# Gate and up of two feed-forwards by seven block products, and down as a pass of its own, in a two-layer diffusion backbone

## The chip, the cores and the metric

The kernel runs on one core of a Trainium2 chip, as one program. The metric is the device time of one execution in microseconds, from the median of several runs. A profile is one further execution that the hardware profiler recorded; its span is the time from its first to its last recorded instruction.

## The reference

The reference is a backbone of two layers over 512 latent tokens and 256 context tokens of width 1024. Layer 0 mixes with a gated MLP and a Hyena convolution, layer 1 with grouped-query attention. Both end in a SwiGLU feed-forward, which is the part that changes. Cut to it:

```python
D_FF = 2816
def swiglu(h, w_gu, w_down):            # w_gu (1024, 5632), w_down (2816, 1024)
    gate, up = jnp.split(h @ w_gu, 2, axis=-1)
    return (jax.nn.silu(gate) * up) @ w_down
...
x = x + g2 * swiglu(modulate(x, norm2_g[layer], sh2, sc2), ffn_w_gu[layer], ffn_w_down[layer])
if not last:
    ctx = ctx + cg2 * swiglu(modulate(ctx, norm2_g[layer], csh2, csc2), ffn_w_gu[layer], ffn_w_down[layer])
return rmsnorm(x, final_g)              # after the last layer
```

`modulate` is an RMS norm whose result is scaled and shifted per column. The feed-forward of layer 0 ("the first" below) works on 768 tokens, six tiles of 128; that of layer 1 ("the second") on the 512 latent tokens, four tiles.

## The kernel before

**Precision.** Every float32 operand of a matrix product is split into a high part, rounded to the format `fp32r`, and a low part, the rest. ScalarE (ACT) makes the high part with a cast, VectorE (DVE) the low part with a subtraction. A product is three matmuls into the same PSUM bank: high by high, high by low, low by high (`mm3`, lines L144, L146 and L148). For weights, `wload` issues a DMA of 512 KB from SyncE's queue (SP, L163) into one of three buffers called `raw`, then casts (`whi`, L166) and subtracts (`wlo`, L167). The ring of three `raw` buffers is used in the order of issue; a load waits until the subtraction that last read its buffer is done. SP's queue is in order as well.

**Filler.** Each `wload` first calls `fill`, which adds one step of a generator: one load of 512 KB of `mod_w` into the same ring (L328) and the matmuls on it (L331) for the conditioning of the next layer. In the first feed-forward 48 such steps are taken.

**A feed-forward.** `norm_hT` takes a token tile at a time: a sum of squares on ACT (L377), a reciprocal root on DVE and GpSimd (POOL, L362), a scaling on DVE (L379), eight transposes on TensorE (L384), scale and shift of the eight 128x128 blocks, four on ACT (L388) and four on DVE (L390), then a cast (L392) and a subtraction (L393) of 128x512, two of each. Its result `hT`, the transposed tokens in high and low parts, has the features on the partitions and the tokens along the columns. Then 11 groups `gi` follow, each of 256 of the 2816 inner columns. A group makes, for each of its two blocks of 128, the gate and the up product over eight k-blocks, with the weights as the stationary and the tokens as the moving operand; the tokens are taken as 384 + 384 columns in the first feed-forward, as 512 in the second (256 + 256 in its first group). Silu on ACT (L964), a multiplication on DVE (L966), the split of the activations (L154, L155), and then at once the group's part of the down product: for each token tile and each half of the 1024 output columns six matmuls of 512 columns (L979), whose bank DVE adds to a sum `fy` in SBUF (L983). In the last group the bank is multiplied by the gate (L906) and added to the residual `xr` (L907). After the second feed-forward comes the final norm (L1147 to L1159), after the first the norm of the attention.

**Order.** The program is one stream per engine, in an order that a scheduler fixed at build time. An engine works its stream in order; semaphores hold an instruction until its operands are there. `project_tm` (L814) is the routine that the mixers' output projections use: all token tiles have a PSUM bank each and the k-blocks of the weights are streamed past them, two k-blocks per load.

## Time and profile before

| what | value |
|---|---|
| time, median of 3 runs | 2107.66 us (2105.82 to 2111.17) |
| time of the profiled execution | 2105.39 us |
| its span | 2103.5 us |
| granted TensorE clock, mean over the span | 0.985 of full speed |
| TensorE matmul busy | 2020.9 us, 96% of the span |
| VectorE, ScalarE, GpSimd busy | 1134.6, 674.6 and 284.8 us |
| first feed-forward, first gate matmul to last down matmul | 869.7 to 1464.1 us |
| second feed-forward, the same | 1726.7 to 2090.0 us |
| end of the span | 2103.5 us |

The profiled execution took 1.9 us more than its span and 2.3 us less than the median of the runs. Busy shares are averages over stages that differ, so what an edit is worth is read from the stage in which it stands. A matmul's recorded duration includes its passage through the array, and matmuls overlap; the pace of a stream is read from one start to the next.

### The profile page before, as it was taken

Reading aid. Unit: us, or ns where it says so; the run is one execution under the profiler, and the core shown is the slowest. Engines: PE = TensorE matmul, PEld = TensorE weight load, DVE = VectorE, ACT = ScalarE, POOL = GpSimd, SP = SyncE. Lnnn points to the kernel's source line nnn. Section 1 sums busy time; section 2 is a strip of 40 time slices with the busy share of each in tenths; the row PEclk is TensorE's granted clock in tenths of the full one; section 3 lists DMA queues with packets and bytes.
Section 4 is the critical chain, followed back from the end, with each engine's and each line's share of the span. In section 5 each row is a group of like instructions: output and inputs, shape, how many; then the busy total and the mean of one; then the engine's idle time right before and its main releaser. Section 6 shows DMA issues by size and latency. Waiting matters only on the chain.

```text
span 2103.5 us, 27501 instructions
## 1 busy us (share of the span) xinstructions
PE 2020.9 (96%) x10875; PEld 1709.1 (81%) x10875; DVE 1134.6 (54%) x1963; ACT 674.6 (32%) x1234; POOL 284.8 (14%) x267
## 2 busy tenths in 40 slices
PE   5899999999999899899999999998989989999997
PEld 2567777899999788788888888997869978888886
DVE  5786173577777742533333333456687644444447
ACT  4654122233333221511111111113567642222222
POOL 3465010012121210200000000003150020000001
PEclk9999999999999999999999999999999999999998
DMA  7664345422222352323333333222220023233331
GB/s 256 217 221 151 108 158 181 168 78 93 79 94 74 109 203 78 121 90 110 118 99 106 120 121 101 62 69 60 61 80 1 31 71 91 81 109 100 91 105 66
DMA packets 170315, 227.77 MB, mean 108 GB/s; under 512 B 8570, under 2 KB 124395, under 8 KB 169931
## 3 DMA queue, kind: packets, MB, share of 16 engines
q1 hardware_dynamic: 169712, 219.95, 33.2%
q0 software_dynamic: 288, 5.90, 0.7%
q8 instruction: 86, 1.41, 0.3%
q14 instruction: 43, 0.34, 0.1%
q10 hardware_dynamic: 186, 0.17, 0.0%
HBM read 204.91 MB, written 21.07 MB: 107 GB/s over the span
## 4 chain that ended last, share of the span: by engine, by line
PE 89%; DMA 4%; DVE 3%; issue 1%; POOL 1%; ACT 1%; SPq 0%; DVEq 0%; POOLq 0%; ACTq 0%
PE pp L144 15%; PE pp L148 15%; PE pp L146 15%; PE pc L979 13%; PE pp L814 11%; PE pc L814 4%; PE pa L331 3%; DMA raw<-in_mod_w 2%; PE pc L144 1%; PE pc L146 1%; PE pc L148 1%; PE pa L148 1%; PE pa L146 1%; PE pa L144 1%; PE pt L1030 1%
## 5 line engine op out<-in xcount | busy, mean ns | idle before, releaser
L166 ACT CAST whi<-raw 128x1024 fp32r<-128x1024 f32 x208 | 216.7, 1051 | 868.0 <-PE pp L146 381.6
L167 DVE TENSOR_TENSOR wlo<-raw,whi 128x1024 fp32r<-128x1024 f32 x208 | 260.8, 1260 | 367.3 <-ACT whi L166 363.8
L144 PE MATMUL pp<-hTh,whi 128*128 128x384 f32 (+2 forms) x1088 | 324.5, 351 | 1.0 <-ACT hTh L392 1.0
L146 PE MATMUL pp<-hTl,whi 128*128 128x384 f32 (+2 forms) x1088 | 323.7, 348 | 0.0
L148 PE MATMUL pp<-hTh,wlo 128*128 128x384 f32 (+2 forms) x1088 | 322.5, 349 | 0.0
L983 DVE TENSOR_TENSOR fy<-pc,fy 128x512 f32<-128x512 f32 x180 | 120.6, 688 | 193.8 <-PE pc L979 193.6
L144 PEld LDWEIGHTS pp<-hTh,whi 128*128 128x128 f32 x1088 | 198.2, 189 | 29.7 <-ACT fa L964 10.9
L148 PEld LDWEIGHTS pp<-hTh,wlo 128*128 128x128 f32 x1088 | 199.7, 189 | 20.4 <-DVE fy L983 4.2
L146 PEld LDWEIGHTS pp<-hTl,whi 128*128 128x128 f32 x1088 | 199.7, 189 | 13.1
L907 POOL TENSOR_TENSOR xr<-xr,nh 128x512 f32<-128x512 f32 x35 | 49.1, 1425 | 915.2 <-DVE nh L906 911.1
L979 PE MATMUL pc<-whi,fasl 128*128 128x512 f32 x440 | 172.3, 392 | 0.2 <-DVE fasl L155 0.2
L979 PE MATMUL pc<-wlo,fash 128*128 128x512 f32 x440 | 172.2, 391 | 0.0
L979 PE MATMUL pc<-whi,fash 128*128 128x512 f32 x440 | 166.2, 394 | 0.0
L144 PE MATMUL pp<-hT,whi 128*128 128x512 f32 (+1 forms) x512 | 135.5, 341 | 0.4 <-ACT whi L166 0.4
L146 PE MATMUL pp<-hT,whi 128*128 128x512 f32 (+1 forms) x512 | 135.7, 340 | 0.0
L148 PE MATMUL pp<-hT,wlo 128*128 128x512 f32 (+1 forms) x512 | 134.8, 340 | 0.0
L979 PEld LDWEIGHTS pc<-whi,fash 128*128 128x128 f32 x440 | 82.1, 188 | 27.1 <-issue 10.1
L331 PE MATMUL pa<-raw,sc 128*32 128x512 f32 x384 | 87.1, 624 | 10.8 <-DMA raw<-in_mod_w 10.7
L979 PEld LDWEIGHTS pc<-wlo,fash 128*128 128x128 f32 x440 | 82.5, 187 | 17.4
L979 PEld LDWEIGHTS pc<-whi,fasl 128*128 128x128 f32 x440 | 82.6, 188 | 16.2 <-DVE fasl L155 0.6
L144 PEld LDWEIGHTS pp<-hT,whi 128*128 128x128 f32 x512 | 79.6, 188 | 15.1 <-issue 2.5
L148 PEld LDWEIGHTS pp<-hT,wlo 128*128 128x128 f32 x512 | 79.6, 189 | 12.0 <-DVE sv L891 0.8
(344 smaller groups left out, 3787.9 us busy)
## 6 DMA issues: line engine op xcount, KB each, us to landing
raw<-in_mod_w SPq DMA_DIRECT2D x96, 512.0 KB
raw<-in_ffn_w_gu SPq DMA_DIRECT2D x88, 512.0 KB
raw<-in_ffn_w_down SPq DMA_DIRECT2D x44, 512.0 KB
raw<-in_even_w_in SPq DMA_DIRECT2D x40, 512.0 KB
G<-G SPq DMA_DIRECT2D x48, 256.0 KB
Gc<-G SPq DMA_DIRECT2D x16, 768.0 KB
raw<-in_even_w_out SPq DMA_DIRECT2D x16, 512.0 KB
dec<-in_k_dec SPq DMA_DIRECT2D x48, 128.0 KB
```

The source lines that it names most:

```text
L144: mm(o, lh, rh, start=start, stop=False)
L146: mm(o, lh, rl, start=False, stop=False)
L148: mm(o, ll, rh, start=False, stop=stop)
L166: self.nc.scalar.copy(hi, raw)
L167: self.nc.vector.tensor_sub(lo, raw, hi.bitcast(F32))
L331: nc.tensor.matmul(ps[32 * j:32 * j + 32, :], self.sc[:, k, :], raw[:, i * 512:(i + 1) * 512], start=k == 0, stop=k == KT - 1, tile_positi ...
L814: self.nc.tensor.matmul(ps, x[:, ts], y[:, a, :], start=k + a == 0 and i == 0, stop=k + a == wk - 1 and i == 2)
L907: (eng or nc.gpsimd).tensor_add(x[:, cs], x[:, cs], tmp)
L979: nc.tensor.matmul(ps, x[:, ts], y[:, 0, cs], start=i == 0 and j == 0, stop=i == 1 and j == 2)
L983: nc.vector.tensor_add(ys[q][:, cs], ps, ys[q][:, cs])
L1030: self.nc.tensor.transpose(ps[:, js], src[:, js], self.eye)
```

## The change

**Gate and up.** The tokens are taken as pairs of tiles, the 1024 features as two halves, and the gate and up weights of one block of 128 inner columns as the two block columns of a 2x2 matrix. The product of two 2x2 block matrices takes eight block products; the changed kernel uses a scheme of seven (that of Strassen, in its form with fewer additions). For each of the 22 blocks `f`, `weight_pairs` loads the gate block and the up block (two loads of 512 KB into the same `raw` ring), forms four sums of halves (two on POOL, two on DVE, each 128x512), and splits 3.5 blocks of 128x1024 worth of operands where the kernel before splits two. `norm_pairs` makes, in place of `hT`, seven operands per pair of tiles: three of them blocks of the tokens as they are, four sums or differences of such blocks (two on DVE, two on POOL), and the high and the low part of each. `gate_up` runs seven products of four k-blocks each, with 384 columns in the first and 256 in the second feed-forward, into four PSUM banks X, Y, Z, W (L1082); adds the banks together on DVE (L1094, L1098, L1099, L1101); applies silu (L1096, L1102) and the multiplications (L1104 on DVE, L1105 on POOL); and stores the two halves of the activation to a DRAM tensor `act` (L1107, SP).

**Down.** It starts when all 22 blocks are stored, with `project_tm` over 22 k-blocks, once for each half of the output columns, all token tiles in PSUM banks. `act` is loaded back through the `raw` ring (L1044) and split; the second feed-forward keeps all 22 split blocks for the second half, the first keeps 12 and loads ten again. The sums in `fy` and DVE's additions to them (L981, L983, L948, L949) go away. `project_tm` works the last four k-blocks of the second half bank by bank, so that the banks finish one after another.

The diff, cut to its core:

```diff
@@ norm_pairs, in place of norm_hT for the feed-forwards
+            for q in pair:
+                nc.scalar.activation(y, x, AF.Square, accum_out=ss)
+                self.rstd(ss, D, EPS)
+                nc.vector.tensor_scalar(y, x, ss, None, op0=ALU.mult)
...
+            put(0, top(h1))
+            put(1, bot(h1))
+            nc.vector.tensor_sub(t1, top(h2), top(h1))
+            nc.vector.tensor_sub(t2, bot(h2), t1)
+            put(3, t1)
+            put(4, t2)
+            nc.gpsimd.tensor_sub(t3, bot(h2), top(h2))
+            nc.gpsimd.tensor_sub(t4, bot(h1), t2)
+            put(5, t3)
+            put(2, bot(h2))
+            put(6, t4)
@@ weight_pairs
+        h0, l0 = split(ra, self.wp, "w", self.wbufs[1])
+        nc.gpsimd.tensor_add(s1, a21, a22)
+        nc.vector.tensor_sub(s2, s1, a11)
+        h1, l1 = split(st, self.wp, "w", self.wbufs[1])
+        nc.gpsimd.tensor_sub(a11, a11, a21)
+        nc.vector.tensor_sub(a12, a12, s2)
+        h2, l2 = split(ra, sp, "s", 2)
+        h3, l3 = split(a22, sp, "v", 1)
@@ gate_up, for f in range(22)
+            prod(X, a11, b11, True, True)
+            nc.scalar.copy(p1, X)
+            prod(W, s1, t1, True, True)
+            nc.scalar.copy(p5, W)
+            prod(Y, s2, t2, True, True)
+            nc.vector.tensor_add(p1, Y, p1)
+            prod(X, a12, b21, False, True)
+            nc.scalar.activation(a[0], X, AF.Silu)
+            prod(Z, s3, t3, True, True)
+            nc.vector.tensor_add(Z, Z, p1)
+            nc.vector.tensor_add(p5, Z, p5)
+            prod(W, s4, b22, False, True)
+            nc.vector.tensor_add(a[1], W, p1)
+            nc.scalar.activation(a[1], a[1], AF.Silu)
+            prod(Z, a22, t4, False, True)
+            nc.vector.tensor_mul(a[0], a[0], Z)
+            nc.gpsimd.tensor_mul(a[1], a[1], p5)
+            for i in range(2):
+                nc.sync.dma_start(acts[f][:, i * n:(i + 1) * n], a[i])
@@ ffn, down
-                        if gi == 0:
-                            nc.vector.tensor_copy(ys[q][:, cs], ps)
-                        elif gi < ng - 1:
-                            nc.vector.tensor_add(ys[q][:, cs], ps, ys[q][:, cs])
+                for cg in range(2):
+                    banks = self.project_tm(lazy, wd, cg * 512, range(ntt), nff, 2 * cg)
+                    for i, ps in enumerate(banks):
+                        self.gated_add(fp, xs[q], ps, gates[q // 4], cg, nc.vector if l and (i == 3 or cg) else None)
```

Three places of the order are shown, all in the second feed-forward. The first is VectorE's stream in the norm. In the kernel before, a piece of it reads as follows (`nxn` is the scaled tile, `nh` a modulated half, `hTl` its low part, `pp` a PSUM bank):

```order
L379 TENSOR_SCALAR nxn_15455<-xr_7602,nss_15454 128x1024
L390 TENSOR_SCALAR nh_15401<-pp_15400,A_2830_15362,modT_7_98 128x128 x2
L393 TENSOR_TENSOR hTl_15361<-nh_15371,hTh_15360 128x4x128
L393 TENSOR_TENSOR hTl_15361<-nh_15383,hTh_15360 128x4x128
L393 TENSOR_TENSOR hTl_15361<-nh_15401,hTh_15360 128x4x128
L390 TENSOR_SCALAR nh_15413<-pp_15412,A_2830_15362,modT_7_98 128x128 x2
```

In the changed kernel the last tile and the operands of the last pair read as follows (`tt` holds a sum of blocks, `Bl` the low part of an operand; the matmuls that open the products need the `Bl` from `nh_2999` of the row marked x2):

```order
L948 TENSOR_SCALAR nxn_15689<-xr_7602,nss_15688 128x1024
L968 TENSOR_TENSOR Bl_15588<-nh_2999_15669,Bh_15587 128x4x128 x2
L959 TENSOR_SCALAR nh_3004_15694<-pp_15695,A_2982_15589,modT_7_98 128x128 x2
L973 TENSOR_TENSOR tt_15717<-nh_3004_15694,nh_2999_15669 128x512
L959 TENSOR_SCALAR nh_3004_15694<-pp_15704,A_2982_15589,modT_7_98 128x128 x2
L974 TENSOR_TENSOR tt_15718<-nh_3004_15694,tt_15717 128x512
L968 TENSOR_TENSOR Bl_15588<-tt_15717,Bh_15587 128x4x128
L968 TENSOR_TENSOR Bl_15588<-nh_3004_15694,Bh_15587 128x4x128
L968 TENSOR_TENSOR Bl_15588<-tt_15718,Bh_15587 128x4x128
L968 TENSOR_TENSOR Bl_15588<-tt_15726,Bh_15587 128x4x128
L968 TENSOR_TENSOR Bl_15588<-tt_15719,Bh_15587 128x4x128
```

A pair now has seven subtractions to low parts in place of four, and two differences of blocks on the same engine.

The second place is VectorE's stream in the steady part of gate and up. In the kernel before, the piece between two runs of `fy` additions reads:

```order
L167 TENSOR_TENSOR wlo_16774<-raw_16771,whi_16773 128x1024
L966 TENSOR_TENSOR fa_16669<-pp_16708,fa_16669 128x512
L167 TENSOR_TENSOR wlo_16810<-raw_16807,whi_16809 128x1024
L155 TENSOR_TENSOR fasl_16735<-fa_16669,fash_16734 128x512
L167 TENSOR_TENSOR wlo_16816<-raw_16813,whi_16815 128x1024
L966 TENSOR_TENSOR fa_16738<-pp_16777,fa_16738 128x512
```

In the changed kernel one block `f` reads (`st` holds two of the sums, `wlo`, `slo` and `vlo` are low parts of weights, `p_` and `fa_` lie in SBUF, `pp` in PSUM):

```order
L1008 TENSOR_TENSOR st_17424<-st_17424,raw_17416 128x512
L1104 TENSOR_TENSOR fa_3235_17187<-fa_3235_17187,pp_17185 128x256
L1012 TENSOR_TENSOR raw_17416<-raw_17416,st_17424 128x512
L1002 TENSOR_TENSOR vlo_17309<-raw_17289,vhi_17308 128x512
L1094 TENSOR_TENSOR p_3256_17318<-pp_17313,p_3256_17318 128x256
L1002 TENSOR_TENSOR slo_17434<-raw_17416,shi_17433 128x1024
L1002 TENSOR_TENSOR wlo_17428<-st_17424,whi_17427 128x1024
L1098 TENSOR_TENSOR pp_17314<-pp_17314,p_3256_17318 128x256
L1099 TENSOR_TENSOR p_3257_17319<-pp_17314,p_3257_17319 128x256
L1002 TENSOR_TENSOR wlo_17550<-raw_17545,whi_17549 128x1024
L1101 TENSOR_TENSOR fa_3255_17317<-pp_17315,p_3256_17318 128x256
```

The eleven instructions of a block stand interleaved with those of the block before it: the low parts and sums of the next weights lie between the additions of the banks.

The third place is SP's queue of loads. In the kernel before, a group of the second feed-forward issues these six:

```order
L163 DMA raw_17312<-in_ffn_w_gu 128x8x128
L163 DMA raw_17344<-in_ffn_w_gu 128x8x128
L163 DMA raw_17381<-in_ffn_w_gu 128x8x128
L163 DMA raw_17413<-in_ffn_w_gu 128x8x128
L163 DMA raw_17449<-in_ffn_w_down 128x1024
L163 DMA raw_17455<-in_ffn_w_down 128x1024
```

In the changed kernel's first half of down it issues, for every two k-blocks, a weight and two activations:

```order
L163 DMA raw_18678<-in_ffn_w_down 128x2x512
L1044 DMA raw_18684<-act_4_2962_15557 128x512
L1044 DMA raw_18693<-act_5_2963_15558 128x512
L163 DMA raw_18720<-in_ffn_w_down 128x2x512
L1044 DMA raw_18726<-act_6_2964_15559 128x512
L1044 DMA raw_18735<-act_7_2965_15560 128x512
```

Each of the three goes to a buffer of its own of the ring, and the next weight needs the buffer of the last one.

## Rows read from the trace of the kernel before

**Rows 1.** the page: busy time by engine, granted clock, chain that ended last

```profile
PE 2020.9 (96%) x10875; PEld 1709.1 (81%) x10875; DVE 1134.6 (54%) x1963; ACT 674.6 (32%) x1234; POOL 284.8 (14%) x267
...
PEclk9999999999999999999999999999999999999998
...
PE 89%; DMA 4%; DVE 3%; issue 1%; POOL 1%; ACT 1%; SPq 0%; DVEq 0%; POOLq 0%; ACTq 0%
```

**Rows 2.** windows by stage: start:end length, busy us by engine, PEclk, DMA share, GB/s

```profile
852.00:869.70 17.70, 11.85 (x67) 6.93 (x65) 14.59 (x34) 13.17 (x30) 2.71 (x3) 0.90 0.77 241
869.70:1464.00 594.30, 594.12 (x3088) 519.91 (x3089) 229.89 (x298) 112.54 (x148) 13.32 (x13) 1.00 0.32 96
1464.00:1474.00 10.00, 4.33 (x23) 3.62 (x22) 9.07 (x15) 7.48 (x16) 8.63 (x8) 0.70 0.32 102
1713.00:1727.00 14.00, 7.34 (x36) 6.18 (x36) 11.19 (x26) 12.10 (x26) 4.62 (x5) 0.76 0.22 75
1727.00:1731.00 4.00, 4.00 (x23) 4.00 (x22) 3.25 (x8) 3.65 (x7) 0.00 (x0) 0.57 0.02 4
1731.00:2090.00 359.00, 358.02 (x1659) 299.36 (x1657) 172.22 (x212) 94.02 (x122) 5.32 (x5) 1.00 0.30 88
```

**Rows 3.** timeline of PE: gate/up with 384, 512 and 256 columns (start, us)

```profile
935.76 0.51 PE L144 MATMUL pp<-hTh,whi 128*128 128x384 f32 x2
...
939.57 0.51 PE L148 MATMUL pp<-hTh,wlo 128*128 128x384 f32 x2
...
1772.72 0.39 PE L148 MATMUL pp<-hTh,wlo 128*128 128x512 f32 x1
...
1774.53 0.39 PE L146 MATMUL pp<-hTl,whi 128*128 128x512 f32 x1
...
1732.72 0.28 PE L146 MATMUL pp<-hTl,whi 128*128 128x256 f32 x1
...
1735.00 0.28 PE L148 MATMUL pp<-hTh,wlo 128*128 128x256 f32 x1
```

**Rows 4.** groups by line and shape, DVE: busy us, mean ns, idle before

```profile
L167 DVE TENSOR_TENSOR wlo<-raw,whi 128x1024 fp32r<-128x1024 f32 x208 | 260.8, 1260 | 367.3 <-ACT whi L166 363.8 <-PE pc L814 2.0
...
L966 DVE TENSOR_TENSOR fa<-pp,fa 128x384 f32<-128x384 f32 x44 | 22.5, 552 | 60.4 <-PE pp L148 60.4
...
L393 DVE TENSOR_TENSOR hTl<-nh,hTh 128x512 fp32r<-128x512 f32 x32 | 21.0, 685 | 4.1 <-ACT hTh L392 3.5
...
L906 DVE TENSOR_TENSOR nh<-pc,gate 128x512 f32<-128x512 f32 x24 | 16.0, 685 | 6.8 <-PE pc L979 4.4 <-PE pc L814 2.0 <-POOL xr L907 0.4
...
L379 DVE TENSOR_SCALAR nxn<-xr,nss 128x1024 f32<-128x1024 f32 x16 | 14.7, 923 | 6.7 <-POOL nss L362 4.0 <-PE pp L384 1.8 <-issue 1.0
...
L390 DVE TENSOR_SCALAR nh<-pp,A,modT 128x128 f32<-128x128 f32 x40 | 13.6, 402 | 0.9 <-issue 0.8 <-ACT nh L388 0.2
...
L1033 DVE TENSOR_TENSOR PTl<-pt,PTh 128x256 fp32r<-128x256 f32 x32 | 13.3, 415 | 0.9 <-ACT PTh L1032 0.9
```

**Rows 5.** groups by line and shape, ACT and POOL

```profile
L166 ACT CAST whi<-raw 128x1024 fp32r<-128x1024 f32 x208 | 216.7, 1051 | 868.0 <-PE pp L146 381.6 <-PE pc L979 120.6 <-PE pc L814 83.3
...
L392 ACT CAST hTh<-nh 128x512 fp32r<-128x512 f32 x32 | 19.0, 625 | 7.1 <-DVE nh L390 7.1
...
L907 POOL TENSOR_TENSOR xr<-xr,nh 128x512 f32<-128x512 f32 x35 | 49.1, 1425 | 915.2 <-DVE nh L906 911.1 <-DVE nss L361 2.8 <-ACT fy L1147 1.4
...
L581 POOL TENSOR_TENSOR ab<-ab,ab 128x256 f32<-128x256 f32 x32 | 27.9, 871 | 22.2 <-DVE ab L576 19.7 <-PE pp L413 1.6 <-DVE rn L603 0.8
```

**Rows 6.** timeline of DVE and POOL, 565 to 571 us

```profile
566.30 1.78 DVE L155 TENSOR_TENSOR Yr0l<-T,Yr0h 128x512 fp32r<-128x512 f32 x1
...
565.33 2.21 POOL L766 TENSOR_TENSOR T<-T,T 128x512 f32<-128x512 f32 x1
```

**Rows 7.** timeline of SP's and PE's queues at 860 us

```profile
860.75 0.33 SPq L328 DMA_DIRECT2D raw<-in_mod_w  x1
...
863.14 1.35 PE L331 MATMUL pa<-raw,sc 128*32 128x512 f32 x4 [4.56 <-DMA raw<-in_mod_w]
```

More of the change, by code (lines that the diff above doesn't have):

```diff
@@ L934, in ffn @@
+    def ffn(self, xs, l):
         nc, A = self.nc, self.A
         ntt = len(xs)
[L936 to L990 removed]
@@ new lines, in gate_up, with prod @@
+    def gate_up(self, fp, sp, b, wgu, acts, n):
+        nc = self.nc
+        b11, b21, b22, t1, t2, t3, t4 = b
+        mm = nc.tensor.matmul
+        def prod(ps, wt, bt, first, last):
+            (wh, wl), (bh, bl) = wt, bt
+            for k in range(4):
+                for i, (x, y) in enumerate(((wh, bh), (wl, bh), (wh, bl))):
+                    mm(ps, x[:, k, :], y[:, k, :], start=first and k == 0 and i == 0, stop=last and k == 3 and i == 2, skip_group_check=not first)
+        for f in range(len(acts)):
+            a11, a12, s1, s2, s3, s4, a22 = self.weight_pairs(sp, wgu, f * P, DFF + f * P)
+            X, Y, Z, W = (self.psA()[:, 0:n] for _ in range(4))
+            a = [self.t(fp, [P, n], F32, f"fa{i}", 2) for i in range(2)]
+            p1 = self.t(fp, [P, n], F32, "p1", 2)
+            p5 = self.t(fp, [P, n], F32, "p5", 2)
+            prod(X, a11, b11, True, True)
[17 more added lines that the diff above has]
+                nc.sync.dma_start(acts[f][:, i * n:(i + 1) * n], a[i])
@@ L1036, in attention_in @@
         nc, A = self.nc, self.A
-        self.hT = self.norm_hT(xs, 1, 1, hp, "hT")
+        with self.pool("an") as yp:
+            self.hT = self.norm_hT(xs, 1, 1, hp, "hT", yp)
         qT = [[[self.t(kvp, [P, 4, P], F32R, f"qT{p}", 8) for p in "hl"] for _ in range(4)] for _ in range(2)]
@@ L1144, in final @@
         if cg == 0:
[L1145 to L1146 removed]
+            self.fss = getattr(self, "fss", {}) | {i: self.t(self.sp, [P, 2], F32, "fss", 4)}
+        ss = self.fss[i]
         nc.scalar.activation(y[:, halves[cg]], x[:, halves[cg]], AF.Square, accum_out=ss[:, cg:cg + 1])
```

165 lines of the change are left out of this document (102 added, 63 removed).

## Prediction

> **What bounds the kernel now.** I read the page first: TensorE is busy 96% of the span, the chain of waits that ended last is 89% TensorE, and the granted clock is at its upper level, 2.4 GHz, in nearly every slice [rows 1]. Busy shares are averages, so the second view is the windows by stage [rows 2]. In the first feed-forward TensorE is busy 594.1 of 594.3 us at full clock, in the second 358.0 of 359.0; VectorE works 230 and 172 us in the same stretches, ScalarE 113 and 94. Both stages are nothing but matmuls in a row, so what they take is number of matmuls times pace, and VectorE has more than half its time to give. The exceptions are the ends. Ahead of the first gate matmul stand a window of 17.7 us with 11.9 us of TensorE work and one of 14.0 us with 7.3; VectorE is busy 14.6 and 11.2 us there. The third view is the pace, in the timeline [rows 3]: from the first to the last row of each stretch, twice 11 steps of 384 columns take 3.81 us, 173 ns each; 8 steps of 512 take 1.81 us, 226 ns each; 19 of 256 take 2.28 us, 120 ns each. The 256-column stream is in the trace only because the second feed-forward's first group is cut in halves, and it is the row that matters most: all of the new gate and up there runs at that width.
>
> **What is removed.** Gate and up before: first feed-forward 22 blocks x 2 parts x 8 k x 3 x 2 column pieces = 2112 matmuls of 384 columns; after, 22 x 7 products x 4 k x 3 = 1848. The difference of 264 at 173 ns is **45.7 us**. Second: 960 of 512 columns and, in the first group, 192 of 256, so 217.0 + 23.0 = 240.0 us; after, 1848 of 256 at 120 ns, 221.8 us: **18.2 us**. Seven eighths would be 30 us of 240; the rest is lost because a matmul of 256 columns is dearer by the column than one of 512 [rows 3]. Down keeps its 1320 matmuls of 512 columns. Conditioning keeps its 48 steps. In all 64 us of TensorE work go away.
>
> The Trainium skill, TensorE: Matmul & The Clock Gate, section Back-to-back issue gap, gives N / 2.4 + 2.5 ns for an isolated matmul at the upper clock: 109, 162.5 and 216 ns for these widths. By that the two terms would be 43 and 27 us. The rows show 11 ns more at each width, a constant that weighs most on narrow matmuls, and they decide.
>
> DVE's 180 additions to `fy` and ten large ones at the end go too; they were hidden and are worth nothing by themselves.
>
> **Gate and up, steady part.** VectorE per block `f`: three subtractions of 1024 columns at 1.26 us, three ops of 512 in SBUF at 0.685, five from PSUM, at 0.415 for 256 columns and 0.552 for 384 [rows 4]. That is 3.78 + 2.06 + 2.08 = 7.9 us against 84 x 0.120 = 10.1 us of TensorE in the second feed-forward, and 8.6 against 84 x 0.173 = 14.5 in the first. ScalarE, with 3.5 casts at 1.05 us per 1024 columns [rows 5] and four ops of a bank that cost no more than the 512-column cast's 0.625 [rows 5], has at most 6.2. POOL has two ops of 512 at 1.43 and one of 256 at 0.87, 3.7 us [rows 5]. So by busy time alone TensorE stays the bound, with 2.2 us to spare in the second feed-forward.
>
> What can use that up is VectorE against POOL. While POOL's op of 2.21 us ran, a VectorE op of 512 columns with both inputs in SBUF took 1.78 us [rows 6] where the same shape takes 0.685 [rows 4]: 1.1 us more; those that read a PSUM bank keep 0.685 (L906, though its partner on POOL follows it closely). If each of POOL's two ops of 512 costs VectorE 1.1 and the one of 256 half of that, a block takes 7.9 + 2.75 = 10.6 us and TensorE waits 0.55 us x 22 = 12 us. But only 5.8 of each 10.1 us are VectorE ops of that kind, so some 1.6 us will be paid, 9.5 in all: hidden, but at 94% in a fixed order of interleaved blocks (second order shown) some waits of TensorE follow. Below, 0; above, 34 us (the second rival). I take **6 us**.
>
> The Trainium skill, SBUF — State Buffer, section SBUF: two separate sides, speaks against this change: GpSimd and VectorE with two SBUF inputs share a port pair under an exclusive lock, and the later one blocks for the whole instruction of the other. The trace agrees in kind (1.78 against 0.685 us); in size it shows half of POOL's time being paid.
>
> In the first feed-forward the engines have 4 us of slack per block, but the ring of three `raw` buffers is shared by two weights and two conditioning loads per block. A load takes 2.4 us from issue to its first matmul [rows 7]. Before, a weight left its buffer after 1.05 + 1.26 us; now the gate block is overwritten in place and stays for cast, POOL's sum, two VectorE ops, a second cast and its subtraction, 1.05 + 1.43 + 0.69 + 0.69 + 1.05 + 1.26 = 6.2 us and whatever it queues for. Two buffers are thus held for half of each 14.5 us, and conditioning matmuls whose load comes late stop the whole TensorE stream, as one did for 4.56 us [rows 7]. Between 0 and 25 us (1.1 us per block); I take **8**.
>
> **The norms.** They stand on the path: TensorE has nothing else then. Second feed-forward, VectorE work before the first product: four scalings at 0.92, 16 modulations at 0.40, and low parts of 0.685, 8 before; after, 14 and four differences, +10 x 0.685 = 6.9 us. The weight sums and splits of the first two blocks go there too, 2 x (3.78 + 3 x 0.685) = 11.7 us where before about three splits of 1.26 did; +7.9. Five low parts come after the first product can start (the first order shown), -3.4. That is 11.4 us on a VectorE that was busy 11.2 of 14.0 us [rows 2]: **+12 us**, between 8 and 16. First feed-forward, six tiles: 21 low parts for 12 and six differences, +15 x 0.685 = 10.3, the weights' +7.9, less 3.4, and 3.1 us of idle VectorE time to absorb some: **+12**, between 6 and 18. The clock's slower stretch after the norm (0.57 granted between 1727 and 1731 us [rows 2], so mostly 1.2 GHz, after a window with TensorE half idle) is paid before as well.
>
> **Down.** Its first matmuls wait for the first weight and activations to be loaded and split: 2.4 + 1.05 + 1.26 us less what the last products cover, 1 to 3 us, twice: **4**. In the second feed-forward's first half, two k-blocks give TensorE 24 x 0.226 = 5.4 us. The loads are 512 KB and twice 256 KB; at the 241 GB/s of the densest window [rows 2] 4.35 us. A buffer is refilled after load, cast and subtraction: at best 2.4 + 1.05 + 1.26 = 4.7 us, and 4.35 + 2.3 + 0.4 = 7.1 where the three loads share the bandwidth (the third order shown). So 0 to 1.7 us for each of 10 such steps; I take the middle, **8 us**. Before, the two down loads of a group stood among four others with 32 us of matmuls to cover them. The first feed-forward has 36 x 0.226 = 8.1 us per step against at most 7.7: hidden. At the hand-over to attention TensorE is busy 4.3 of 10 us already [rows 2]; six banks now finish within some 4 us where they came 2.7 us apart, 0 to 5, **2 us**. The last tail is shorter by 0 to 2: **-1**.
>
> **Sum.** -64 + 6 + 8 + 12 + 12 + 4 + 8 + 2 - 1 = -13 us on the profiled execution's 2105.4, so 2092; the median of the runs stands 2.3 us higher, so **2094 us**.
>
> **Rivals.**
> *All engines keep up* (20%): only the norms and the hand-overs are paid, -64 + 24 + 4 = -36, 2072 us. For it: VectorE has slack of 20% or more and ScalarE and SP far more. Against: fixed orders, and rings of three.
> *VectorE becomes the bound in the second feed-forward* (15%): each of POOL's 3.7 us blocks it wholly, so a block takes 7.9 + 3.7 = 11.6 us, TensorE waits 1.5 x 22 = 34 in place of 6: 2122 us, slower. It decides from 10.1 us of VectorE per block on; the row of 1.78 us speaks for it, the PSUM readers against it.
> *The ring starves TensorE* (12%): 25 and 17 us at the two places in place of 8 and 8, -13 + 26: 2120, slower. For it, the 4.56 us wait; against, 96 and 88 GB/s in these stages [rows 2], far from the 241 of the densest window.
> *Narrow matmuls run faster or the norms hide behind the mixers' tail* (6%): -50 us or more, 2055.
>
> **How the numbers follow.** My case (47%) is 2094 with its own range of 2076 to 2106. About 0.3% (6 us) is what a measurement can tell from no change, so under 2101.3 is faster, over 2114 slower. Faster: 0.36 of my 0.47, the first rival's 0.20, the last's 0.06: 0.62. Slower: 0.03 + 0.12 + 0.10 = 0.25. The rest, 0.13, is the same. The range of 2064 to 2123 leaves out the last rival and the upper ends of the two slow ones.
>
> **What would show.** The first product matmul about 12 us after the last transposes' place of before, twice; 1848 matmuls at 173 and 120 ns starts; gaps on TensorE in the second feed-forward before L1082 released by `slo`, `vlo` or `wlo` (VectorE) rather than by DMA; in its first down half waits of L813 on `raw` loads every 5 to 7 us. The prediction fails if VectorE is above 10 us per block, or if the banks' additions on VectorE are late for the products that reuse a bank.

## The result, and the profile after

The changed kernel takes 2156.06 us (median of 4 runs, 2153.79 to 2158.18), the kernel before 2108.5 us beside it: a ratio of 1.0225, with a 95% interval of 1.0207 to 1.0243. The change made the kernel slower by 2.25%, where 2094 us and a range up to 2123 had been forecast.

The page of the changed kernel answers to [rows 1] and [rows 2]. First its busy times, granted clock and chain, and two of its DMA issues with the median time from issue to landing (the page of before gave no landing times for this queue):

```profile
PE 1982.5 (92%) x11307; PEld 1690.3 (79%) x11307; DVE 1256.9 (58%) x2106; ACT 796.1 (37%) x1455; POOL 479.5 (22%) x409
...
PEclk9999999999999999699999999998999979999999
...
PE 69%; DMA 11%; DVE 9%; issue 4%; POOL 4%; ACT 3%; SPq 0%; POOLq 0%; DVEq 0%; ACTq 0%
...
raw<-in_mod_w SPq DMA_DIRECT2D x96, 512.0 KB, 4.1
raw<-in_ffn_w_gu SPq DMA_DIRECT2D x88, 512.0 KB, 3.8
```

TensorE did get less work, 1982.5 us busy for 2020.9, but its share of the chain fell from 89% to 69%: DMA, VectorE and GpSimd stand in the chain now. The windows by stage (columns as in [rows 2]) say where. In order: first norm, first gate and up, first down, the way into the attention, second norm, second gate and up, second down:

```profile
851.10:897.50 46.40, 18.47 (x71) 8.97 (x70) 36.48 (x62) 26.35 (x51) 19.40 (x15) 0.64 0.32 102
897.50:1286.00 388.50, 369.28 (x2033) 329.03 (x2033) 202.10 (x251) 124.57 (x183) 85.64 (x66) 0.99 0.42 133
1286.00:1466.20 180.20, 180.20 (x794) 146.74 (x793) 62.78 (x67) 47.47 (x54) 11.55 (x9) 1.00 0.45 150
1466.20:1476.00 9.80, 0.25 (x2) 0.09 (x2) 9.72 (x17) 5.41 (x10) 8.05 (x6) 0.77 0.41 107
1722.60:1747.20 24.60, 5.92 (x31) 4.92 (x29) 21.29 (x35) 14.56 (x29) 11.46 (x9) 0.60 0.07 22
1747.20:2013.70 266.50, 237.35 (x1858) 228.55 (x1857) 182.23 (x246) 108.92 (x184) 82.24 (x64) 0.99 0.35 104
2013.70:2143.30 129.60, 124.84 (x525) 97.74 (x523) 47.59 (x58) 37.91 (x56) 8.99 (x8) 0.99 0.39 132
```

The first down pass is matmuls in a row, 180.2 of 180.2 us. The second gate and up is not: TensorE's own 1848 x 0.120 = 221.8 us are spread over 266.5. VectorE is busy 182 of these, 68%, so it is not out of time either. Something waits in a circle.

All kernels of this study can be set beside each other by the starts of the matmuls that bound a stage (last matmul of the mixer's projection, first and last product, last down matmul, last output matmul of the attention, and so on; end of span for the tail). In us, each from its own profiled execution; before and the changed kernel stand first, the others are explained in the experiments:

| kernel | norm 1 | gate/up 1 | down 1 | to end of attention | norm 2 | gate/up 2 | down 2 | tail |
|---|---|---|---|---|---|---|---|---|
| before | 19.0 | 594.2 with down | | 248.9 | 14.0 | 363.1 with down | | 13.7 |
| changed | 46.5 | 388.4 | 180.0 | 256.4 | 24.8 | 266.5 | 129.3 | 9.9 |
| own_ring | 47.0 | 389.8 | 180.0 | 253.8 | 29.2 | 244.4 | 127.0 | 9.9 |
| sums_on_vector | 46.6 | 386.9 | 180.5 | 255.4 | 25.3 | 239.8 | 129.0 | 10.0 |
| no_reload | 47.1 | 390.4 | 180.0 | 255.4 | 27.8 | 228.6 | 128.7 | 10.0 |
| filler_down | 44.6 | 327.3 | 214.5 | 294.7 | 24.7 | 269.0 | 129.4 | 10.5 |
| ring_vector | 46.4 | 389.1 | 179.9 | 255.2 | 28.0 | 228.3 | 126.2 | 10.0 |
| square_aside | 38.9 | 389.9 | 180.1 | 255.0 | 24.6 | 268.3 | 128.0 | 9.9 |
| mod_buffer | 44.5 | 384.0 | 182.7 | 255.8 | 24.8 | 266.3 | 131.4 | 9.9 |
| all_edits | 36.8 | 388.0 | 183.3 | 255.7 | 21.1 | 232.0 | 131.4 | 9.9 |
| kept_last | 46.5 | 388.3 | 179.9 | 253.5 | 24.8 | 267.9 | 128.9 | 9.9 |
| sums_late | 39.2 | 398.8 | 180.2 | 255.8 | 20.2 | 278.7 | 128.6 | 9.9 |
| all_edits2 | 36.8 | 388.0 | 183.2 | 252.5 | 21.1 | 232.8 | 120.5 | 9.9 |

From before to changed: +27.5 in the first norm, 568.4 - 594.2 = -25.8 in the first feed-forward's body, +7.5, +10.8, 395.8 - 363.1 = +32.7 in the second's body, -3.8. That is 48.9 of the 49.5 us between the two spans. A stretch that a kernel's edits leave alone is not the same to the last digit: between such kernels the first gate and up goes from 388.3 to 390.4 us and the way to the end of the attention from 253.8 to 256.4, so differences of that size say nothing by themselves.

**How a block of the second gate and up waits.** Timeline of the changed kernel, one turn of it, from a pair of weight loads to the next (start, us, engine; in brackets the engine's idle time before the op, and what ended it):

```profile
1863.51 1.01 SPq L994 DMA_DIRECT2D raw<-in_ffn_w_gu  x2
...
1867.61 1.05 ACT L1001 CAST whi<-raw 128x1024 fp32r<-128x1024 f32 x1 [3.64 <-DMA raw<-in_ffn_w_gu]
...
1869.40 1.67 POOL L1007 TENSOR_TENSOR st<-raw 128x512 f32<-128x512 f32 x1 [8.25 <-DMA raw<-in_ffn_w_gu]
...
1871.10 1.21 DVE L1008 TENSOR_TENSOR st<-st,raw 128x512 f32<-128x512 f32 x1 [1.19 <-POOL st L1007]
...
1872.39 1.78 POOL L1011 TENSOR_TENSOR raw<-raw,raw 128x512 f32<-128x512 f32 x1 [0.63 <-DVE st L1008]
...
1874.21 1.06 ACT L1001 CAST shi<-raw 128x1024 fp32r<-128x1024 f32 x1 [4.18 <-POOL raw L1011]
...
1875.30 1.23 DVE L1002 TENSOR_TENSOR slo<-raw,shi 128x1024 fp32r<-128x1024 f32 x1 [0.24 <-ACT shi L1001]
```

The two loads are issued from 1863.5 us on; the gate block is there at 1867.6, the up block at 1869.4, where GpSimd had waited 8.25 us for it. Then the sums and splits follow one another through GpSimd, VectorE, GpSimd, ScalarE and VectorE, until at 1876.5 the last reader is done and the second buffer of the pair is free for its next load. One load of the next pair waits for this, the other for a split that ends somewhat earlier (1874.7). So this turn takes 13.0 us, and no op in this chain is released by TensorE. The waits of TensorE in this stage (us in total, times, longest) show the late end of it, the banks' additions that stand behind the sums in VectorE's stream:

```profile
PE pp L1082 <- DVE fa L1104: 12.2, 12, 2.2
PE pp L1082 <- DVE p L1099: 6.9, 6, 2.1
PE pp L1082 <- DVE fa L1101: 4.6, 8, 1.3
```

A block's first products start 10.1 us apart twice, while weights loaded during the norm last, and from then on 12.1 us in the mean (18 blocks, 10.6 to 14.0).

### The profile page after: what moved, and what is told of

Its sections match the earlier page's. It is cut to its first block, busy times and chain, and to the rows that moved or that the text cites. A ratio compares the mean times of both kernels' runs of the same rounds, so it can differ in the third digit from the quotient of the medians.

```text
span 2153.0 us, 29558 instructions
## 1 busy us (share of the span) xinstructions
PE 1982.5 (92%) x11307; PEld 1690.3 (79%) x11307; DVE 1256.9 (58%) x2106; ACT 796.1 (37%) x1455; POOL 479.5 (22%) x409
## 4 chain that ended last, share of the span: by engine, by line
PE 69%; DMA 11%; DVE 9%; issue 4%; POOL 4%; ACT 3%; SPq 0%; POOLq 0%; DVEq 0%; ACTq 0%
PE pp L813 19%; PE pp L1082 13%; PE pc L813 6%; DMA raw<-in_ffn_w_gu 5%; PE pp L144 5%; PE pp L148 5%; PE pp L146 5%; PE pa L330 3%; DMA raw<-in_ffn_w_down 2%; POOL st L1007 2%; DMA raw<-in_mod_w 1%; DVE raw L1012 1%; PE pc L144 1%; PE pc L146 1%; PE pc L148 1%
## 5 line engine op out<-in xcount | busy, mean ns | idle before, releaser
L166 ACT CAST whi<-raw 128x1024 fp32r<-128x1024 f32 x120 | 126.2, 1051 | 383.6 <-PE pc L813 126.6
L1082 PE MATMUL pp<-Bh,whi 128*128 128x384 f32 (+1 forms) x704 | 222.0, 318 | 7.4 <-DVE fa L1101 4.6
L1082 PE MATMUL pp<-Bh,wlo 128*128 128x384 f32 (+1 forms) x704 | 220.2, 313 | 6.1 <-DVE wlo L1002 6.1
L1082 PE MATMUL pp<-Bl,whi 128*128 128x384 f32 (+1 forms) x704 | 219.2, 311 | 2.5 <-DVE Bl L968 2.5
L1082 PEld LDWEIGHTS pp<-Bh,whi 128*128 128x128 f32 x704 | 134.4, 191 | 34.3 <-issue 15.9
L1082 PEld LDWEIGHTS pp<-Bh,wlo 128*128 128x128 f32 x704 | 134.8, 191 | 9.6 <-DVE wlo L1002 9.3
L1082 PEld LDWEIGHTS pp<-Bl,whi 128*128 128x128 f32 x704 | 134.5, 191 | 3.3 <-DVE Bl L968 3.3
L1082 PE MATMUL pp<-Bh,shi 128*128 128x384 f32 (+1 forms) x352 | 111.3, 316 | 14.0 <-DVE fa L1104 12.2
L330 PE MATMUL pa<-raw,sc 128*32 128x512 f32 x384 | 88.7, 645 | 26.1 <-DMA raw<-in_mod_w 25.8
L1082 PE MATMUL pp<-Bl,shi 128*128 128x384 f32 (+1 forms) x352 | 109.4, 311 | 0.0
L1082 PE MATMUL pp<-Bh,slo 128*128 128x384 f32 (+1 forms) x352 | 109.2, 310 | 0.0
L813 PE MATMUL pp<-whi,fkl 128*128 128x512 f32 x256 | 101.2, 396 | 1.0 <-DVE fkl L155 0.2
L762 POOL TENSOR_TENSOR T<-T,T 128x512 f32<-128x512 f32 (+1 forms) x32 | 34.5, 1090 | 266.4 <-DVE T L761 265.3
## 6 DMA issues: line engine op xcount, KB each, us to landing
raw<-act SPq DMA_DIRECT2D x32, 384.0 KB, 4.0
```

Of the source, the lines that this page charges most:

```text
L166: self.nc.scalar.copy(hi, raw)
L330: nc.tensor.matmul(ps[32 * j:32 * j + 32, :], self.sc[:, k, :], raw[:, i * 512:(i + 1) * 512], start=k == 0, stop=k == KT - 1, tile_positi ...
L762: nc.gpsimd.tensor_add(t1, t1, t2)
L813: self.nc.tensor.matmul(ps, x[:, ts], y[:, a, :], start=k + a == 0 and i == 0, stop=k + a == wk - 1 and i == 2)
L1082: mm(ps, x[:, k, :], y[:, k, :], start=first and k == 0 and i == 0, stop=last and k == 3 and i == 2, skip_group_check=not first)
```

## Experiments

**Ring or engines: three kernels on the second gate and up.** The first gives its weights a ring of four buffers.

```diff
-            raw = self.t(self.wp, [P, KT, P], F32, "raw", self.wbufs[0])
+            raw = self.t(sp, [P, KT, P], F32, "graw", 4) if self.layer else self.t(self.wp, [P, KT, P], F32, "raw", self.wbufs[0])
```

> In the second feed-forward alone the gate and up weights get a ring of four buffers of their own in place of their share of the three raw buffers. Theory A (a weight holds its buffer for some 6.8 us and the next load then takes 3.8 to 5 us to land, and with three buffers that loop sets the 12.1 us per block): the stretch from the first to the last gate/up matmul falls from 266.5 us to about 225 to 235, and the whole time by 30 to 40 us, to about 2118 us. Theory B (VectorE and GpSimd block each other, so that VectorE's additions come late): the stretch stays above 255 us and the whole time within 10 us of 2156.

Measured: 2138.34 us over 4 runs, a ratio of 1.0142 (1.0125 to 1.0159) to before. The stretch fell from 266.5 to 244.4 us, about half of the excess over 221.8. So the ring is a cause and not the only one; blocks are 11.0 us apart now. In the second norm 4.4 us were lost again. A turn, from the timeline of this kernel:

```profile
1859.96 1.23 DVE L1002 TENSOR_TENSOR slo<-graw,shi 128x1024 fp32r<-128x1024 f32 x1 [1.94 <-ACT shi L1001]
...
1861.21 1.01 SPq L994 DMA_DIRECT2D graw<-in_ffn_w_gu  x2
...
1865.51 1.29 POOL L1007 TENSOR_TENSOR st<-graw 128x512 f32<-128x512 f32 x1 [6.66 <-DVE fa L1102]
...
1866.84 1.22 DVE L1008 TENSOR_TENSOR st<-st,graw 128x512 f32<-128x512 f32 x1 [1.46 <-POOL st L1007]
...
1868.13 1.80 POOL L1011 TENSOR_TENSOR graw<-graw,graw 128x512 f32<-128x512 f32 x1 [0.63 <-DVE st L1008]
...
1869.96 1.05 ACT L1001 CAST shi<-graw 128x1024 fp32r<-128x1024 f32 x1 [3.59 <-POOL graw L1011]
...
1871.04 1.23 DVE L1002 TENSOR_TENSOR slo<-graw,shi 128x1024 fp32r<-128x1024 f32 x1 [1.94 <-ACT shi L1001]
```

From `slo` to the next `slo` 11.08 us pass, and the load is still in the turn. The pair of loads is issued at 1861.21 us, as `slo` ends (1861.19); by the trace's semaphore records the first of them, the up block that GpSimd's sum reads, has landed at 1865.35, and the sum starts 0.16 us later. The row names an addition of VectorE as the releaser, which ended at about the same time. But in 18 of the last 20 sums of this stage the start is 0.16 us after a load's landing, while the distance to VectorE's op changes. So with four buffers, too, an up block is loaded only when `slo`, the last reader of the gate block before, is done. What the fourth buffer changed is that the up block now comes first of its pair and lands 4.1 us after its issue; in the turn above it came second, 5.1 us after its issue. VectorE's op of 512 columns takes 1.22 us in the turn for 0.685 [rows 4] while GpSimd works, and GpSimd's 1.80 for 1.43 [rows 5] while VectorE does.

The second kernel leaves the ring alone and gives GpSimd's ops to VectorE, in both feed-forwards.

```diff
-        nc.gpsimd.tensor_add(s1, a21, a22)
+        nc.vector.tensor_add(s1, a21, a22)
...
-        nc.gpsimd.tensor_sub(a11, a11, a21)
+        nc.vector.tensor_sub(a11, a11, a21)
...
-            nc.gpsimd.tensor_mul(a[1], a[1], p5)
+            nc.vector.tensor_mul(a[1], a[1], p5)
```

> GpSimd's two weight sums and its product per block go to VectorE, in both feed-forwards; the ring stays. Theory B (blocking between the two engines costs the time): the stretch of the second feed-forward's gate and up falls from 266.5 to below 245 us, since VectorE's work, 7.9 + 2 x 0.685 + 0.415 = 9.7 us per block, stays under 10.1. Theory A (the ring's loop): the hold of a buffer shortens only by the difference of the operations, some 1.3 + 1.8 - 2 x 0.7 = 1.7 us of 12.1 per block, so the stretch falls to about 235 to 250 or, if VectorE is then late for the banks, does not fall at all.

Measured: 2129.29 us in one run, the stretch at 239.8 us, 26.7 less. More work on VectorE, the engine that seemed in danger, made the stage shorter, which fits a turn with two changes of engine fewer and no blocking. Taken alone it would fit both theories; the third kernel tells them apart. It loads the weights of the second gate and up once and leaves out the loads of the other 21 blocks, so its second feed-forward computes with the weights of block 0 throughout.

```diff
+            if self.layer and ca:
+                raws = self.raws
+                break
...
+        sd = self.t(sp, [P, KT, P], F32, "sd", 1) if self.layer else ra
-        nc.gpsimd.tensor_sub(a11, a11, a21)
-        nc.vector.tensor_sub(a12, a12, s2)
-        h2, l2 = split(ra, sp, "s", 2)
+        nc.gpsimd.tensor_sub(sd[:, 0:4, :], a11, a21)
+        nc.vector.tensor_sub(sd[:, 4:8, :], a12, s2)
+        h2, l2 = split(sd, sp, "s", 2)
```

> In the second feed-forward the weights of block 0 are loaded once and used for all 22 blocks; every sum, cast and subtraction per block is still made, into a buffer of its own. So loads and ring are gone and all engine work is kept. The output of the second feed-forward is computed with the wrong weights. Theory A: the stretch falls from 266.5 us to about 222 to 228, TensorE's own 221.8 us. Theory B: it stays above 250 us, since VectorE and GpSimd do the same work as before.

Measured: 2122.77 us in one run; the window of the stage reads

```profile
1753.60:1982.20 228.60, 226.59 (x1859) 225.89 (x1858) 183.93 (x246) 112.71 (x184) 83.80 (x63) 0.99 0.10 32
```

VectorE is as busy as in the changed kernel (183.9 and 182.2 us), GpSimd too (83.8 and 82.2), and TensorE loses nothing after the first block: 10.1 us each. So the contention of the two engines does not cost TensorE time by itself. It does so only inside a turn that also holds loads and buffers; which of these two is not told apart here, since this kernel leaves out both. The fourth corner is both edits together, for the second feed-forward (the first keeps GpSimd).

> Second feed-forward: the ring of four buffers and VectorE in place of GpSimd for the two sums and the product. With the ring alone a block took 10.9 us, the length of a loop that goes VectorE, GpSimd, VectorE, GpSimd, ScalarE, VectorE; with VectorE alone 10.3 to 11.3 us. If these are two loops of their own, both are now under TensorE's 10.1 us, and the stretch of gate and up falls to 226 to 230 us, 37 to 40 us less than in the changed kernel. If VectorE is the bound as such, at 9.7 us of work per block, it stays at 236 us or more.

Measured: 2116.96 us in one run, the stretch at 228.3 us, blocks 10.1 us apart. The number expected came, though the text above takes the loop that the ring alone leaves for one of engines only, and the load was in it. The four corners are 266.5, 244.4 with the ring, 239.8 with the sums on VectorE, 228.3 with both: either edit gives 22 to 27 us, both 38, and what is left over 221.8 is mostly the first block, 14.7 us long, whose first 4 us run at the clock's lower level, 1.2 GHz (0.50 granted between 1750.5 and 1754.5 us), after a norm with TensorE mostly idle, and the last one of 12.0 us.

**The first feed-forward's conditioning.** Its steps are taken out of norm and gate/up.

```diff
-            self.filler = self.adaln_steps([(1, 0), (1, 1), (1, 2)])
             self.ffn(xs, 0)
...
+            if not l:
+                self.filler = self.adaln_steps([(1, 0), (1, 1), (1, 2)])
             with self.pool("fact", "right") as rp, self.pool(f"ffb{l}") as fp:
```

> The 48 steps of conditioning are taken out of the first feed-forward's norm and gate/up; 22 of them run in its down pass and the rest stands alone behind it, so the whole time says little. Theory A (the shared ring starves TensorE in the first feed-forward too): the stretch from first to last gate/up matmul falls from 388.5 us by more than the some 48 us that the conditioning's matmuls took themselves, to 322 to 328 us; and the wait from the mixer's last matmul to the first product, 46.4 us, falls to about 34 us, because no load of conditioning stands between two loads of weights in SP's queue. Theory B: the gate/up stretch falls by the 48 us alone, to about 340 us, and the norm stays at 44 us or more.

Measured: 2168.06 us in one run; the first gate and up took 327.3 us with every block but the first 14.6 us apart. 61.1 us went away. In the changed kernel 40 steps stand there, in 32 places of TensorE's stream at some 1.2 us each, and TensorE's listed waits in it are 11.2 us for loads of `mod_w` and 8.1 us for split weights and copies, 19 us together. That conditioning costs them is shown by this kernel, and that it does so through the ring by the next. The norm lost only 1.9 us of its 46.5, so conditioning is not most of what lengthened it. The steps moved cost more where they went (214.5 in down, 294.7 to the end of the attention).

A buffer of its own for conditioning inside gate and up, and for the activations of the second down pass:

```diff
+                own = getattr(self, "modpool", None)
-                raw = self.t(self.wp, [P, 1024], F32, "raw", self.wbufs[0])
+                raw = self.t(own, [P, 1024], F32, "mraw", 1) if own else self.t(self.wp, [P, 1024], F32, "raw", self.wbufs[0])
...
-                    raw = self.t(self.wp, [P, 1024], F32, "raw", self.wbufs[0])[:, 0:2 * n]
+                    raw = self.t(fp, [P, 2 * n], F32, "araw", 4) if l else self.t(self.wp, [P, 1024], F32, "raw", self.wbufs[0])[:, 0:2 * n]
```

> Conditioning gets one buffer of its own inside the first feed-forward's gate and up, so that the weights there have the three raw buffers to themselves, and no step of it stands in the norm. In the second feed-forward's down pass the activations get a ring of four buffers of their own. If the shared ring is the cause, the first gate/up stretch falls from 388.4 us to 327 us plus 44 steps of some 1.05 us, 373 to 378, and the second down from 129.3 to 120 to 123 us. If the conditioning's matmuls wait for the memory whatever the ring, the first stays above 383; if transfers set the down pass, the second stays above 126.

Measured: 2152.38 us in one run. TensorE's listed waits in the first gate and up are 0.3 us where the changed kernel's were 19.3, so the shared ring was what made it wait. But the stretch is 384.0 us, only 4.4 less. That is the number of the second answer and not its cause: the conditioning itself takes more of TensorE here, 45 steps in 47 places, for 40 in 32. In the changed kernel two steps often stand together and take no longer than one alone; with a single buffer none do:

```profile
1012.86 1.06 PE L330 MATMUL pa<-raw,sc 128*32 128x512 f32 x8
...
1003.69 1.05 PE L330 MATMUL pa<-mraw,sc 128*32 128x512 f32 x4
```

(The first row is of the changed kernel, two steps; the second of this one, one step.) At some 1.2 us each the 15 more places cost back most of the 19 us. The second down pass did not gain but lost 2 us. In the kernel with all edits, below, two rows show why: the pass's first matmul waited 9 us for the first activation, whose load into the new buffer is issued only at 1975.47 us, after the last product of gate and up (1974.3). The new buffers come from a pool that opens when that of gate and up closes.

```profile
1975.47 18.64 SPq L1050 DMA_DIRECT2D araw<-act  x14
...
1983.54 2.08 PE L813 MATMUL pp<-whi,feh 128*128 128x512 f32 x4 [8.97 <-ACT feh L154]
```

**The norms.** The squares go aside, and VectorE makes the last residual additions of the first feed-forward.

```diff
-                    nc.scalar.activation(y, x, AF.Square, accum_out=ss)
+                    junk = big[1][:, 5:7, :, j * P:(j + 1) * P]
+                    nc.scalar.activation(junk, x.rearrange("p (c f t) -> p c f t", c=2, t=P), AF.Square, accum_out=ss)
...
-self.gated_add(fp, xs[q], ps, gates[q // 4], cg, nc.vector if l and (i == 3 or cg) else None)
+self.gated_add(fp, xs[q], ps, gates[q // 4], cg, nc.vector if cg or l and i == 3 else None)
```

> In both norms the sum of squares writes its squares over an operand that is not made yet, in place of the one buffer of the scaled tile, and behind the first feed-forward the last residual additions go from GpSimd to VectorE. If the norm's time is the chain through that one buffer (square, root, scaling, transposes, and only then the next square), the first norm falls from 46.5 us to 34 to 40, the second from 24.8 to about 20. If it is VectorE's work and its waits for weights, both stay within 2 us. If GpSimd's six additions in a row, 9.6 us, hold back the attention, the stretch from the first feed-forward's last matmul to the attention's last falls from 256.4 us by 3 to 6.

Measured: 2148.05 us in one run. The first norm fell by 7.6 us to 38.9, though the first block behind it takes 2.3 us more (20.0 for 17.7); the second did not fall (24.6), and the way through the attention fell by 1.4, no more than kernels without the edit differ. In the changed kernel's first norm TensorE's rows show the chain through the one buffer, waits for the scaled tile `nxn` before the transposes of four of the six tiles (18.1 us in all), and three for conditioning (9.8 us). Here the waits for `nxn` are 3.1 us:

```profile
873.14 1.92 PE L330 MATMUL pa<-raw,sc 128*32 128x512 f32 x4 [5.41 <-DMA raw<-in_mod_w]
...
882.48 1.94 PE L953 MATMUL pp<-eye,nxn 128*128 128x128 f32 x8 [5.52 <-DVE nxn L948]
...
896.60 1.30 PE L953 MATMUL pp<-eye,nxn 128*128 128x128 f32 x5 [5.70 <-DVE nxn L948]
```

Then the buffer of the weight sums is put where it is free only after the norm.

```diff
-        st = self.t(sp, [P, KT, P], F32, "st", 1)
+        st = self.t(self.late, [P, KT, P], F32, "st", 1)
```

> The buffer of the two weight sums lies in memory that the norm's pool frees, so that no sum of weights is made before the norm is over; casts and low parts of the first blocks can still be. If the weight work ahead of the norm's in the streams of VectorE, ScalarE and GpSimd costs the norm time, the first norm falls from 46.5 us by 6 to 10 and the second from 24.8 by 4 to 8, and some of it comes back as a wait between the first two products, inside the gate/up stretch. If the norm is a chain of its own, both stay within 2 us.

Measured: 2162.51 us in one run. Norms of 39.2 and 20.2 us, 7.3 and 4.6 less, and gate/up stretches 10.4 and 12.2 us longer. So the weight work ahead of the norm does cost the norm, but it is needed at once behind it: the first blocks take 26.2 and 23.0 us for 17.7 and 14.7.

**The way into the attention.** The first feed-forward keeps its last activations for the second half, and reloads early ones.

```diff
-pool, tag, bufs = (ep, "fe", early) if k < early else (rp, "fk", kept - early) if k < kept else (rp, "fo", 3)
+pool, tag, bufs = (ep, "fe", early) if k < early else (rp, "fo", 3) if k < early + nff - kept else (rp, "fk", kept - early)
...
-                    for k in range(kept, nff):
+                    for k in range(early, early + nff - kept):
```

> In the first feed-forward's down pass the activations of blocks 1 to 10 are reloaded for the second half and those of 0 and 11 to 21 are kept, where the changed kernel keeps 0 to 11 and reloads 12 to 21. The last four k-blocks then need no load, and the order of the last matmuls is 12 per bank, bank after bank. If the attention's late start comes from banks that finish together, the stretch from the first feed-forward's last matmul to the attention's last output matmul falls from 256.4 us to the 248.8 of the kernel before, within 2. If it comes from the residual additions, rope tables and weights on VectorE, it stays above 254.

Measured: 2154.12 us in one run, 253.5 us for 256.4. Five of the six banks are now read 2.4 to 3.1 us apart, where in the changed kernel three were read at once at 1462.4 us, but only 2.9 of the 7.5 us came back, and own_ring, which leaves this part alone, has 253.8 as well. Clearer is TensorE's wait for the attention's first scaled tile: 9.5 or 9.6 us in the changed kernel, own_ring, sums_on_vector, no_reload and ring_vector, which share this part, 7.0 here, 5.0 before. So spreading the banks gave some 2.5 us: between the two answers. With the additions on VectorE as well (all_edits2) the wait is 6.6 us and the stretch 252.5, 3.6 over before. What holds these was not tested. The rows show that the kernel before scales two tiles for the attention's norm ahead of its last down matmul (1458.6 and 1462.2 for 1463.8 us), while in all_edits2 eight ops on rope tables, 2.7 us, stand in VectorE's stream between the last residual addition and the first scaling.

**All edits together.** Ring, sums on VectorE in the second feed-forward, squares aside, conditioning's buffer, activations' ring, residual additions.

> All edits of the three other kernels of this set together. If the losses are independent, their gains add: 38 us in the second gate and up, 6 to 10 in the first norm, 4 in the second, 10 to 15 in the first gate and up, 6 to 9 in the second down, 3 to 6 ahead of the attention, in all 67 to 82, so 2074 to 2089 us against 2108 before. If one loss gives way to another, the time stays above 2095 us.

Measured: 2111.09 us over 10 runs, a ratio of 1.0013 (1.0000 to 1.0026): the kernel before is reached and not passed, and the 2074 to 2089 us of independent gains are missed. The two gains of the first norm add up (36.8 us for 46.5), but the first block behind it takes 23.0 us for 17.7; the second norm is 3.7 us shorter and its first block 4.6 longer (19.3 for 14.7), so nothing is won there. The second gate and up keeps 34.5 of its 38.2 us, the second down pass stays as late as in mod_buffer (131.4). The last kernel mends the late activations (`if l and k > 3` for the ring) and adds the kept ones of above.

> All edits as before, with two mended: the first four activations of the second down pass come through the raw ring, whose buffers are free before the pass begins (its first matmul waited 9 us for them), and the kept activations are the last ones, as in the kernel above. If both work, 8 us fall off the second down pass and 5 off the way to the attention: 2111 - 13 = 2098 us, under the 2108 of the kernel before. If the wait of 9 us has another cause, the time stays above 2104.

Measured: **2099.93 us** over 10 runs, a ratio of **0.9962** (0.9951 to 0.9973) to the kernel before. The second down pass takes 120.5 us; 519 of its 528 matmuls lie in the stretch, 519 x 0.2263 = 117.4. This version beats both, the kernel before by 0.4%.

## Why the prediction was wrong

**Right.** The saving of TensorE: blocks run 14.6 and 10.1 us apart wherever they are fed (filler_down, ring_vector), as 84 matmuls at 173 and 120 ns, so 64 us of work are gone. The estimate of 70 us that comes out of the formula of the Trainium skill (2.5 ns a matmul over the bare columns; TensorE: Matmul & The Clock Gate, section Back-to-back issue gap) is not reached. The second norm, +12 forecast, +10.8 measured; which ops make it up was not tested. The first down pass is hidden.

**Right in size, in part by luck.** Down in the second feed-forward lost 129.3 - 522 x 0.2263 = 11.2 us for the 8 and half of the 4 (six of the 528 matmuls run before the stretch; counted with it, as in the sum below, 9.8). Some 6.5 us are in the first half, in short waits for split operands about every 6.1 us, as forecast. But the first matmul did not wait: it starts 0.12 us after the last product. Instead the second half's first matmul waited 2.8 us until VectorE had read a bank:

```profile
PE pp L813 <- DVE nh L905: 2.8, 1, 2.8
```

In all_edits2, where most activations have a ring of their own, 3.1 us are left. The forecast of 8 was the middle of a range whose lower end used a load of 2.4 us, which no run shows (below).

**The step that failed** is the steady part of gate and up, in the sentence that TensorE stays the bound with 2.2 us to spare and 6 us are lost. 44.7 us were (266.5 - 221.8). I compared each engine's busy time per block with TensorE's, found VectorE at 94% at worst (measured, 182.2 / 22 = 8.3 of 10.1 us, 82%), and looked for the loss in its contention with GpSimd. The bound is instead a turn of waits: load, GpSimd, VectorE, GpSimd, ScalarE, VectorE, and the buffer's next load. Its members were all priced in the prediction, but added up only for the first feed-forward, where conditioning shares the ring; for the second I took a ring that no other load shares to be free. With the figures that stood there, 6.2 us of hold and 2.4 us of load, a turn is 8.6 us and would have fitted into 10.1. The load was misread too. The two rows of [rows 7] do not belong together: by the semaphore that it waits for, the matmul at 863.14 us reads the load issued at 854.99, which landed at 863.10. The load of the row, issued at 860.75, landed at 866.01, 5.3 us after its issue, and its matmuls stand at 867.17:

```profile
854.99 0.33 SPq L328 DMA_DIRECT2D raw<-in_mod_w  x1
...
867.17 1.05 PE L331 MATMUL pa<-raw,sc 128*32 128x512 f32 x4
```

Of the 305 weight loads of 512 KB in that trace none landed in under 3.3 us, and the median is 3.9. With 3.9 the same sum is 6.2 + 3.9 = 10.1 us: nothing to spare. The turn shown above is 13.0 us: 0.6 until the second load is issued, 5.1 for the load, 0.2 to GpSimd's start, and 7.1 for the five ops, for which the rows of before give 1.43 + 0.69 + 1.43 + 1.05 + 1.26 = 5.9; most of the difference is the blocking (1.67 and 1.78 for 1.43, 1.21 for 0.69).

Of the signs that the prediction names, the waits of TensorE before L1082 are hardly ever released by `slo`, `vlo` or `wlo` (1.2 us), but by the banks' additions (L1104, L1099 and L1101, 23.7 us), which is the second of its signs of failing.

**The rivals.** The one with VectorE as the bound and the one with the starving ring were each given one place and one price. The ring is the mechanism, at a place where that rival had put no price; GpSimd's ops make its turn longer. VectorE never was the bound: with its full work and GpSimd's it left TensorE unhurt once no load stood in the turn (no_reload). The Trainium skill (SBUF — State Buffer, section SBUF: two separate sides) calls the two engines' shared port an exclusive lock, under which the later op is blocked. The rows agree: VectorE's op that began at 1871.10 us ended at 1872.31, 0.55 us after GpSimd's product in L1105 (1871.03 to 1871.76). So an op pays what is left of the other's, 0.4 to 0.5 us for most ops that meet here, not GpSimd's whole 3.7 us per block; it matters because it lies on the turn.

**Terms that were mis-sized.** The first gate and up lost 19 us for the 8 taken; the bound of 25 held, and the cause was the shared ring as stated (listed waits of 19.3 us, 0.3 with a buffer of its own for conditioning). The first norm was +27.5 for +12, outside its bounds of 6 to 18. I had counted VectorE's work. The chain through the one `nxn` buffer (7.6 us in square_aside, 5.3 with the first block behind it) was not in the sum, and the weights' share was counted as VectorE's time only, without the waits for loads and for GpSimd that come with it in an engine's order. Some 6 of the 17.8 us that all_edits2 still pays there (36.8 against 19.0) are over the 12 and not resolved further. The way into the attention was +7.5 for +2: banks that finish together were seen, but what remains after they are spread (3.6 us in all_edits2) stays open. The tail gained 3.8 for 1.

Added up: the second gate and up 35 us over its term (38.7, of which before lost 3.5 as well), the first 11, the first norm 15.5, the way into the attention 5.5; under their terms the second norm by 1, down and hand-overs by 2, the tail by 3. That is 61 of the 62 us between forecast and result.

## What to carry to other kernels

When an edit makes a load's buffer serve in several steps, find the op that releases the next block's load. If it is the last reader of the block before, add up the whole turn, issue to landing and then every op to that last reader on whichever engine it runs, and set it against TensorE's time per block; busy shares, even of 68% on the next engine, say nothing of it. One buffer more helps only as far as the load then waits for an earlier block: with four in place of three the turn still held the load, and fell from 12.1 to 11.0 us. Before pricing a load from two rows of a timeline, make sure that the second row reads that load and not an earlier one, and compare with other loads of the same size. Fewer multiplications are worth only what the narrower matmuls and the work around them leave: 64 us of matmuls saved gave 8 us of time, and those only after the turn was broken and the waits around it were shortened.

## What had not been expected of the hardware

Weight loads of 512 KB land 3.8 and 4.1 us after their issue as the medians of the two lines shown from the changed kernel's page; one of the kernel before took 8.1 us. In the first norm of the changed kernel one GpSimd op of 512 columns took 4.02 us, 1.43 being its usual time [rows 5], while VectorE ran a row of four ops with two SBUF inputs to 890.35 us, each in its usual time; so it is not always VectorE that pays, and one op can be held up by several:

```profile
887.45 4.02 POOL L978 TENSOR_TENSOR tt<-nh 128x512 f32<-128x512 f32 x1 [0.41 <-ACT Bh L967]
...
887.86 0.68 DVE L974 TENSOR_TENSOR tt<-nh,tt 128x512 f32<-128x512 f32 x1
888.46 0.69 DVE L968 TENSOR_TENSOR Bl<-tt,Bh 128x512 fp32r<-128x512 f32 x1
889.06 0.68 DVE L968 TENSOR_TENSOR Bl<-nh,Bh 128x512 fp32r<-128x512 f32 x1
889.66 0.69 DVE L968 TENSOR_TENSOR Bl<-tt,Bh 128x512 fp32r<-128x512 f32 x1
```
